# A two-layer GLA and neighbourhood-attention encoder: instructions ordered by a timeline simulation instead of the scheduler's own model

## The chip, the cores and the metric

The kernel runs on one core of a Trainium2 chip. The metric is the device time of one execution in microseconds; shorter is better. The core has TensorE (matmuls, PE in the profile; its weight loads are PEld), VectorE (DVE), ScalarE (ACT), GpSimd (POOL) and SyncE (SP), which issues nearly all DMA transfers here. Each engine works through its own list of instructions strictly in order; semaphores make it wait for other engines and for transfers. The kernel's operands, tiles and work are the same before and after the change; what differs is the order of each list.

## The reference

Two layers over 256 tokens and 16 meta tokens (272 in all), D = 2048, float32, batch 1. In each layer one projection gives the inputs of four GLA heads (bidirectional gated linear attention, 128 key and 256 value channels, chunks of 64) and of 16 heads of two-dimensional neighbourhood attention (NA, 64 channels, a window of 4 by 16 on a grid 64 wide, plus the meta tokens):

```python
proj = h @ w_in            # q,k,v,r,decay of GLA | q,k,v of NA
gla = _gla_mixer(q, k, v, r, gate_lr, w_up, b_up, norm_w)
na  = _na_mixer(nq, nk, nv, rel_bias)
h = _layer_norm(alpha * h + concat(gla, na) @ w_out, ln1_w, ln1_b)
h = _layer_norm(alpha * h + square(relu(h @ w_ff1)) @ w_ff2, ln2_w, ln2_b)
```

The MLP is 8192 wide. The meta tokens are dropped from the output, which is (1, 256, 2048).

## The kernel before

**Tiles and matmuls.** Activations lie transposed, 128 channels by 272 tokens, as 16 tiles x0 to x15 (y and u later on). Each float32 operand is split into a high part in the fast matmul format (fp32r) and a low rest; a product takes three matmuls (high by high, high by low, low by high), written as one of 512 columns and one of 256 where both parts of x lie beside each other. A weight tile is 128 x 1024 floats, 512 KB. L192 loads it on SP's queue into `raw` (3 buffers), L215 casts it to `wh` on ACT, L216 computes `wl` = raw - wh on DVE (4 buffers of each). `weights()` asks for tiles two ahead (`lead`), in the fixed order of `order()`. Some 770 tiles go through in all.

**Loops.** `by_m` walks over output tiles and accumulates over k in one PSUM bank (`eight`, L250, and `sixteen`, L262). `by_k` (L302, or `dense`, L312) walks over k and fills four or eight banks at once; layer 0 begins with it, two groups g of four banks for each k, since x arrives in pairs of tiles. There the program calls `load_x` for each pair (L431 loads `xraw`, 272 KB, 3 buffers; ACT and DVE split it). Layer 1 begins with it too, on the x that the second layer norm of layer 0 leaves.

**Side work.** GLA, NA, the layer norms and the gates are Python generators in two queues, `fg` and `bg`. After every group of main matmuls `pump` runs a step or more of them, so that their instructions are written between the main ones. In detail, as far as the steps below need it:

- Start: `load_gates` loads the decay weights (L451, two of 196 KB; L452, 256 KB), `consts` (L89 to L98) the vectors, identity and masks; L768 loads the bias `nb` of an NA pair of heads (352 KB), eight a layer.
- NA: softmax on ACT, DVE and POOL (L760 ends the meta tokens' part, `nms`), transposes by TensorE (L805, L806, L808), the product with v (L851, L858).
- GLA: L716 to L720 are the output matmuls, from `parts` (split by L337 on ACT and L338 on DVE) and `am` (L343).
- Layer norm: sums by TensorE (L983 makes one from `sp`), then `newton` (L576 to L578) makes `rs`, the reciprocal deviation; `ln_wide` (L1085) subtracts the mean `mu` and multiplies by `rs`, two tiles at a time; gain and bias follow on ACT (L1075) or POOL; `renew` splits the result into the next x (L337, L338). The first projections after it don't wait for it: they use the x from before the norm, and `fix` (L1121 to L1123) applies the norm to their result `fx`.
- End: `ln_out` turns the result back to tokens by rows: L1143 transposes (`turn`, four matmuls a block, eight blocks), L1156 the sums for each token, L1163 to L1167 and `newton` the deviation, L1148 subtracts the mean, L1182 scales and adds on DVE, and DMAs write the output.

**What sets the order.** The program's calls give each instruction a place in program order. The tile framework then schedules: it goes through the program with a model of how long things take, and picks for each engine which of the instructions whose inputs are ready in its model comes next, with program order as the tie-break. `issue_after` holds an instruction back until another one, here the last `wl` of the weights, has been placed; all side work and no transfer of `load_x`, L192 or L224 stands under it:

```python
raw = self.xr.tile([P, 2, L], F32, name="xraw", tag="xraw", bufs=3)      # L430
self.nc.sync.dma_start(raw, self.i["xT"][:, k:k + 2, :])                 # L431
...
with self.tc.issue_after(self.wl):                                       # in step()
    self.wants[q[0]] = bool(next(q[0]))
...
self.asked = nc.sync.dma_start(raw[:, c], ap[:, c]).ins                  # L192
self.nc.scalar.copy(h, r)                                                # L215
self.wl = self.nc.vector.tensor_tensor(lo, r, h.bitcast(F32), ALU.subtract).ins  # L216
```

Of the kernel before, what the change touches and what calls it, by code (L numbers as in the profile page):

```python
# [1259 lines left out]
def program(nc, arrays):  # L1260
    ins = {n: nc.dram_tensor(f"in_{n}", a.shape, mybir.dt.from_np(a.dtype), kind="ExternalInput").ap()
           for n, a in arrays.items()}
    out = nc.dram_tensor("out_0", (T, D), F32, kind="ExternalOutput").ap()
    with tile.TileContext(nc) as tc, ExitStack() as ctx:
        nc.scalar.preload_act_table_set("natural_log_exp_and_others")
        k = Trunk(ctx, tc, ins, out)
        for l in range(DEPTH):
            k.layer(l)
# [13 lines left out]
```

## Time and profile before

| | us |
|---|---|
| median of 3 runs | 2315.6 (2315.4 to 2317.69) |
| span of the profiled execution, the only time given of it | 2314.3 |
| busy: TensorE, VectorE, ScalarE, GpSimd | 2300.4, 1519.4, 1224.6, 160.4 |

The span runs from the first to the last instruction of the profiled execution and lies 1.3 us under the median. A row of a group or of the timeline reads: start in us (timeline only), duration in us, engine, line, operation, output <- inputs, shapes, how many in a row of that kind, and in brackets the idle time of the engine ahead of it and what ended it. Names carry no buffer numbers there. Adjacent matmuls overlap, so that a row's duration is longer than the time until the next one starts.

### The profile page before, as it was taken

How to read it: one execution, taken by the hardware profiler on the slowest of the kernel's cores; microseconds unless marked ns; L12 is line 12 of the kernel's file. 1: busy time of each engine (PE TensorE's matmuls, PEld its weight loads, DVE VectorE, ACT ScalarE, POOL GpSimd, SP SyncE). 2: the span in 40 equal slices, each digit the busy share in tenths (PEclk: the TensorE clock that was granted, in tenths of full speed). 3: DMA queues.
4: the chain of work that ended last, by engine and by line, in shares of the span. 5: the costliest groups of instructions: out<-in, count | busy, mean ns of one | idle time of the engine just before them, and what ended most of it. 6: DMA issues, size and time to landing. Idle time of an engine off the chain costs nothing.

```text
span 2314.3 us, 45228 instructions
## 1 busy us (share of the span) xinstructions
PE 2300.4 (99%) x18420; PEld 2186.8 (94%) x18420; DVE 1519.4 (66%) x2392; ACT 1224.6 (53%) x2096; POOL 160.4 (7%) x245
## 2 busy tenths in 40 slices
PE   9999999999999999999999999999999999999998
PEld 9999999999999999999999899989988888888888
DVE  5588778875544455547576788788866455666654
ACT  5666665564433344444456766655654334555443
POOL 0023210100000000000020122200100000000000
PEclk9999999999999999999999999999999999999999
DMA  8556665555566666555555566666666666666664
GB/s 263 162 164 185 200 197 177 174 180 177 181 182 178 179 181 181 177 181 181 177 179 165 174 180 204 213 185 191 188 192 193 196 189 195 193 193 221 194 199 138
DMA packets 129824, 431.65 MB, mean 187 GB/s; under 512 B 14792, under 2 KB 23496, under 8 KB 129616
## 3 DMA queue, kind: packets, MB, share of 16 engines
q1 hardware_dynamic: 127024, 421.95, 60.1%
q10 hardware_dynamic: 2592, 6.82, 0.8%
q8 instruction: 144, 2.36, 0.4%
q14 instruction: 64, 0.52, 0.1%
HBM read 420.32 MB, written 8.39 MB: 185 GB/s over the span
## 4 chain that ended last, share of the span: by engine, by line
PE 79%; DVE 3%; ACT 1%; issue 1%; DMA 0%; POOL 0%; DVEq 0%; ACTq 0%; POOLq 0%; SPq 0%
PE mm L250 44%; PE mm L262 30%; PE mm L302 2%; PE mm L312 1%; DVE wl L216 1%; PE bg L312 0%; ACT wh L215 0%; PE bg L302 0%; DMA raw<-in_win 0%; DVE acc L1085 0%; PE bg L851 0%; DVE S L615 0%; ACT ns L756 0%; PE bg L983 0%; PE bg L470 0%
## 5 line engine op out<-in xcount | busy, mean ns | idle before, releaser
L216 DVE TENSOR_TENSOR wl<-raw,wh 128x1024 fp32r<-128x1024 f32 (+1 forms) x770 | 936.3, 1223 | 619.8 <-ACT wh L215 518.4
L215 ACT CAST wh<-raw 128x1024 fp32r<-128x1024 f32 (+1 forms) x770 | 805.4, 1048 | 753.2 <-PE mm L250 360.1
L250 PE MATMUL mm<-x,wh 128*128 128x272 f32 (+3 forms) x4544 | 805.3, 294 | 0.0
L250 PEld LDWEIGHTS mm<-x,wh 128*128 128x128 f32 x4544 | 646.8, 188 | 15.4 <-DVE gtn L577 0.3
L250 PE MATMUL mm<-x,wl 128*128 128x272 f32 (+3 forms) x2432 | 519.6, 284 | 0.0
L250 PEld LDWEIGHTS mm<-x,wl 128*128 128x128 f32 x2432 | 390.8, 188 | 0.0
L250 PE MATMUL mm<-y,wh 128*128 128x272 f32 (+1 forms) x1440 | 235.0, 285 | 0.0
L250 PEld LDWEIGHTS mm<-y,wh 128*128 128x128 f32 x1440 | 199.7, 188 | 0.1
L262 PE MATMUL mm<-x,wh 128*128 128x512 f32 x832 | 193.8, 390 | 0.0
L262 PEld LDWEIGHTS mm<-x,wh 128*128 128x128 f32 x832 | 154.3, 188 | 31.0
L250 PE MATMUL mm<-u,wh 128*128 128x272 f32 (+1 forms) x1056 | 172.1, 285 | 0.0
L262 PE MATMUL mm<-y,wh 128*128 128x512 f32 x688 | 162.2, 389 | 0.0
L262 PEld LDWEIGHTS mm<-y,wh 128*128 128x128 f32 x688 | 128.7, 188 | 26.5
L250 PE MATMUL mm<-y,wl 128*128 128x272 f32 (+1 forms) x720 | 146.4, 284 | 0.0
L250 PEld LDWEIGHTS mm<-u,wh 128*128 128x128 f32 x1056 | 146.3, 188 | 0.0
L262 PE MATMUL mm<-u,wh 128*128 128x512 f32 x496 | 118.3, 391 | 0.0
L250 PEld LDWEIGHTS mm<-y,wl 128*128 128x128 f32 x720 | 112.5, 188 | 0.0
L262 PEld LDWEIGHTS mm<-u,wh 128*128 128x128 f32 x496 | 90.9, 188 | 17.7
L250 PE MATMUL mm<-u,wl 128*128 128x272 f32 (+1 forms) x528 | 107.3, 284 | 0.0
L262 PEld LDWEIGHTS mm<-x,wl 128*128 128x128 f32 x832 | 98.4, 188 | 2.0
L262 PE MATMUL mm<-x,wl 128*128 128x256 f32 x832 | 98.8, 276 | 0.0
L262 PEld LDWEIGHTS mm<-y,wl 128*128 128x128 f32 x688 | 84.2, 188 | 2.8
(285 smaller groups left out, 2288.7 us busy)
## 6 DMA issues: line engine op xcount, KB each, us to landing
raw<-in_wff SPq DMA_DIRECT2D x512, 512.0 KB, 3.8
raw<-in_win SPq DMA_DIRECT2D x190, 512.0 KB, 4.3
raw<-in_wout SPq DMA_DIRECT2D x64, 512.0 KB, 4.2
hop<-nt ACTq DMA_DIRECT2D x16, 384.0 KB, 2.3
np<-hop SPq DMA_DIRECT2D x64, 96.0 KB, 4.6
nb<-in_nab SPq DMA_DIRECT2D x16, 352.0 KB, 4.9
xraw<-in_xT SPq DMA_DIRECT2D x7, 272.0 KB, 5.5
out<-out SPq DMA_DIRECT2D x5, 256.0 KB, 3.4
```

Source lines behind the costliest of these rows:

```text
L215: self.nc.scalar.copy(h, r)
L216: self.wl = self.nc.vector.tensor_tensor(lo, r, h.bitcast(F32), ALU.subtract).ins
L250: mm(o, lhsT=self.block(w, j), rhs=rhs, start=first and not i, stop=last and i == len(TURNS[once]) - 1)
L262: self.nc.tensor.matmul(o, lhsT=self.block(both[j // 8][low], j % 8), rhs=rhs, start=first and not i + j, stop=bool(last and i and j == 15 ...
L302: self.nc.tensor.matmul(ps[g + m][:, :n], lhsT=self.block(parts[p][0], 4 * j + m if first else 2 * m + j), rhs=acts[k + j][parts[p][1]][:, ...
L312: self.nc.tensor.matmul(o, lhsT=self.block(both[low], i), rhs=rhs, start=not low and k + i % 2 == 0, stop=k == DC - 2 and i % 2 == 1 and n ...
```

## The change

One argument of the context under which the whole program is written:

```diff
-    with tile.TileContext(nc) as tc, ExitStack() as ctx:
+    with tile.TileContext(nc, schedule_with_timeline_sim=True) as tc, ExitStack() as ctx:
```

The scheduler now takes the times at which it thinks that engines are free and operands ready from a timeline simulation rather than from its own model. It still picks from the same instructions under the same dependencies. The lists of all engines differ from before, in places by a row, in places by dozens. Three places follow; a row is the line, the operation, output <- inputs with buffer numbers, the shape of the output, and xN for N equal ones in a row.

SyncE's queue at the start of the program, behind the transfers of the first tiles. Each `raw` of 128x1024 is one tile of weights: here those of k = 2, k = 4 and k = 6, two each (groups of banks 0 and 1). Before:

```order
L192 DMA raw<-in_win 128x1024
L431 DMA xraw<-in_xT 128x544
L192 DMA raw<-in_win 128x1024 x2
L431 DMA xraw<-in_xT 128x544
L192 DMA raw<-in_win 128x1024 x2
L431 DMA xraw<-in_xT 128x544
L192 DMA raw<-in_win 128x1024 x2
```

And now:

```order
L192 DMA raw<-in_win 128x1024
L431 DMA xraw<-in_xT 128x544 x3
L451 DMA gw_628<-in_wup 98x512
L192 DMA raw<-in_win 128x1024
L451 DMA gw_629<-in_wup 98x512
L452 DMA gw_630<-in_wlr 128x512
L89 DMA vec<-in_vec 128x2x66
L192 DMA raw<-in_win 128x1024
L91 DMA ident<-in_ident 128x128
L93 DMA sel<-in_sel 98x2
L95 DMA qmask<-in_qmask 16x48
L768 DMA nb<-in_nab 128x704
```

Behind these follow one `raw`, three more `xraw` and three `raw`; the first of those three is the first tile of k = 6. The gate weights, constants and `nb` stood behind all tiles of x before.

VectorE at the second layer norm of layer 0, up to the instruction that makes `rs` (L578). Before:

```order
L1058 TENSOR_TENSOR var_14829<-bg_14826,tn_14831 128x272
L1085 TENSOR_TENSOR acc_4774<-acc_4774,mu_14832 128x544
L1122 SCALAR_TENSOR_TENSOR fx_14877<-mu_14832,wb_14876,mm_14756 128x272
L576 SCALAR_TENSOR_TENSOR tn_14831<-var_14829,eps_656,rs_14830 128x272
L1085 TENSOR_TENSOR acc_4774<-acc_4774,mu_14832 128x544
L577 SCALAR_TENSOR_TENSOR tn_14831<-tn_14831,rs_14830 128x272
L1085 TENSOR_TENSOR acc_4774<-acc_4774,mu_14832 128x544
L578 SCALAR_TENSOR_TENSOR rs_14830<-tn_14831,rs_14830 128x272
L216 TENSOR_TENSOR wl_14929<-raw_14927,wh_14928 128x4x2x128
```

And now:

```order
L1085 TENSOR_TENSOR acc_4774<-acc_4774,mu_14832 128x544 x2
L1058 TENSOR_TENSOR var_14829<-bg_14826,tn_14831 128x272
L216 TENSOR_TENSOR wl_14929<-raw_14927,wh_14928 128x4x2x128
L1085 TENSOR_TENSOR acc_4774<-acc_4774,mu_14832 128x544
L576 SCALAR_TENSOR_TENSOR tn_14831<-var_14829,eps_656,rs_14830 128x272
L1121 COPY wb_14916<-mm_14845 128x2
L216 TENSOR_TENSOR wl_14963<-raw_14961,wh_14962 128x4x2x128
L1085 TENSOR_TENSOR acc_4774<-acc_4774,mu_14832 128x544
L577 SCALAR_TENSOR_TENSOR tn_14831<-tn_14831,rs_14830 128x272
L1122 SCALAR_TENSOR_TENSOR fx_14917<-mu_14832,wb_14916,mm_14845 128x272
L578 SCALAR_TENSOR_TENSOR rs_14830<-tn_14831,rs_14830 128x272
```

One more L1085 and one L1122 stand ahead of these rows, and L578 comes behind two low parts of weights (L216) that used to follow it.

TensorE in layer 0, where the main loop goes over y with `by_k` and L808 turns `nms`, the meta tokens' part of an NA pair. Before:

```order
L805 MATMUL bg<-ident,nv_2208 128x128 x2
L806 MATMUL bg<-ident,nr_2209 128x128
L302 MATMUL bg<-y_1925,wh 128x272 x2
L302 MATMUL bg<-y_2023,wh 128x272
L808 MATMUL bg<-ident,nms 128x128
L302 MATMUL bg<-y_2023,wh 128x272
L302 MATMUL bg<-y_1925,wl 128x272
```

And now:

```order
L302 MATMUL mm<-y_1925,wh 128x272 x2
L302 MATMUL mm<-y_2023,wh 128x272 x2
L302 MATMUL mm<-y_1925,wl 128x272
L808 MATMUL bg<-ident,nms 128x128
L302 MATMUL mm<-y_2023,wl 128x272
L851 MATMUL bg<-np,v_4817 64x128 x2
L851 MATMUL bg<-np,v_4816 64x128 x4
```

L808 now stands 27 main matmuls further back, just ahead of the L851 of the same head pair.

## The prediction

> **What bounds the kernel now.** I read the page first: busy time of the engines, and the chain of work that ended last.
>
> ```profile
> span 2314.3 us, 45228 instructions
> PE 2300.4 (99%) x18420; PEld 2186.8 (94%) x18420; DVE 1519.4 (66%) x2392; ACT 1224.6 (53%) x2096; POOL 160.4 (7%) x245
> PE 79%; DVE 3%; ACT 1%; issue 1%; DMA 0%; POOL 0%; DVEq 0%; ACTq 0%; POOLq 0%; SPq 0%
> ```
>
> TensorE is busy for 2300.4 of 2314.3 us, and the chain lies on it. So 13.9 us are all that a new order could win, unless it made the matmuls themselves shorter, and it changes none of them. The next view gives the busy time in stretches (columns: stretch, length, busy of the five engines with counts, granted clock, DMA share, GB/s).
>
> ```profile
> core 0: us, PE busy (x) PEld busy (x) DVE busy (x) ACT busy (x) POOL busy (x), PEclk, DMA share, GB/s
> 0.00:50.00 50.00, 48.79 (x379) 48.79 (x380) 27.26 (x38) 27.91 (x45) 3.15 (x18) 1.00 0.86 271
> 400.00:1200.00 800.00, 799.98 (x6528) 799.75 (x6527) 458.99 (x607) 362.09 (x508) 13.87 (x17) 1.00 0.60 180
> 2300.00:2314.00 14.00, 8.14 (x60) 7.01 (x58) 6.56 (x15) 3.23 (x8) 2.52 (x2) 0.97 0.41 150
> ```
>
> Of the 13.9 us, 1.21 lie before the first matmul and 5.9 in the last 14 us, behind the last matmul for the greater part. From 400 to 1200 us TensorE misses 0.02 us. The rest, some 6.8 us, is a dozen short gaps. A reordering of the long middle can win nothing there, and the question is whether it opens gaps. So I went through the places where TensorE has little in hand: the start, each gap, the two layer norms that feed a matmul, and the tail.
>
> **The change part by part: the start.** The order rows of the SyncE queue show that in front of the third pair of weight tiles (k = 6) now stand six xraw transfers instead of two, the three of the gate weights, vec, ident and the first nb.
>
> ```profile
> raw<-in_win SPq DMA_DIRECT2D x190, 512.0 KB, 4.3
> nb<-in_nab SPq DMA_DIRECT2D x16, 352.0 KB, 4.9
> xraw<-in_xT SPq DMA_DIRECT2D x7, 272.0 KB, 5.5
> ...
> gw<-in_wup SPq DMA_DIRECT2D x4, 196.0 KB
> raw<-in_win SPq DMA_DIRECT2D x3, 256.0 KB, 4.5
> ...
> head<-in_head SPq DMA_DIRECT2D x2, 264.0 KB, 2.9
> gw<-in_wlr SPq DMA_DIRECT2D x2, 256.0 KB, 5.6
> ```
>
> Up to and including the first tile of k = 6 the queue held: head 2 x 264, three raw of 256, five raw of 512, two xraw of 272; that is 4400 KB or 4.51 MB. Now it holds head 528, raw 768, raw 5 x 512, xraw 6 x 272, gate weights 196 + 196 + 256, vec and ident 66 + 64 (from their shapes) and nb 352: 6618 KB or 6.78 MB. When that tile came, and when TensorE wanted it:
>
> ```profile
> 11.61 1.05 ACT L215 CAST wh<-raw 128x1024 fp32r<-128x1024 f32 x1 [1.41 <-DMA raw<-in_win]
> ...
> 18.36 1.05 ACT L215 CAST wh<-raw 128x1024 fp32r<-128x1024 f32 x1 [1.10 <-DMA raw<-in_win]
> ...
> 23.05 0.65 PE L302 MATMUL mm<-x,wh 128*128 128x272 f32 x4
> ...
> 2.00:46.00 44.00, 44.00 (x345) 44.00 (x344) 24.94 (x36) 25.19 (x44) 1.68 (x11) 1.00 0.92 289
> 12.00:14.00 2.00, 2.00 (x18) 2.00 (x17) 1.23 (x1) 0.66 (x1) 0.00 (x0) 1.00 0.98 366
> ```
>
> The cast at 18.36 waited for this tile, so 4.51 MB had landed by then: counted from 2.0 us, 277 GB/s. The cast at 11.61 waited for the second tile of k = 2, which the rows place at 2.65 MB: 276 GB/s. The mean from 2 to 46 us is 289 GB/s at a DMA share of 0.92; scaled to a share of 1, that is 314, and I take 301, halfway between, as the quick end. The new landing is then 2.0 + 6.78 MB / 289 GB/s = 25.46 us, the cast of 1.05 ends at 26.5, and TensorE wants the tile at 23.05: **+3.5 us**, with 277 GB/s +4.5, with 301 +2.5. The second tile of k = 2 and both of k = 4 come some 0.4 to 0.7 us late by the same sum, which is part of the same lag. Behind k = 6 the lag does not grow: two tiles and an xraw (1.33 MB) in the 5.9 us of their 48 matmuls (0.1225 each, 799.98 us by 6528) are 225 GB/s, less than the queue carries. The gate weights, constants and nb that cause it are themselves wanted later; at their old places, behind the weights, they cost nothing.
>
> The Trainium skill speaks against this delay: DMA: Bandwidth & Descriptors, section "Where 436 GB/s comes from", puts the limit of one core's reads from HBM at about 358 GB/s, and by that figure as an estimate the tile would land at 20.9 us and be cast by 22.0, before it is wanted; no window over the whole start shows such a rate here, only the one at 12 us.
>
> **Second layer norm, 1195 to 1214 us.** DVE's order rows put two L1085, two L216, one L1121 and one L1122 more ahead of L578, which makes rs.
>
> ```profile
> 1195.47 0.72 DVE L1085 TENSOR_TENSOR acc<-acc,mu 128x544 f32<-128x544 f32 x1
> 1196.11 0.44 DVE L577 SCALAR_TENSOR_TENSOR tn<-tn,rs 128x272 f32<-128x272 f32 x1
> ...
> 1197.10 0.44 DVE L578 SCALAR_TENSOR_TENSOR rs<-tn,rs 128x272 f32<-128x272 f32 x1
> 1197.45 1.22 DVE L216 TENSOR_TENSOR wl<-raw,wh 128x1024 fp32r<-128x1024 f32 x1
> ...
> 1208.26 0.65 DVE L338 TENSOR_TENSOR x<-acc,x 128x272 fp32r<-128x272 f32 x1
> ...
> 1209.46 0.43 DVE L338 TENSOR_TENSOR x<-acc,x 128x272 fp32r<-128x272 f32 x1
> ...
> 1209.99 1.67 PE L302 MATMUL mm<-x,wh 128*128 128x272 f32 x12
> ...
> 1212.51 0.73 PE L302 MATMUL mm<-x,wh 128*128 128x272 f32 x4 [0.73 <-DVE fx L1122]
> ```
>
> An L1085 takes 0.64 us from its start to the next; two are 1.3, two L216 2.4, L1122 some 0.44 (the 128x272 shape of L578): 4.2 us, so rs ends at 1201.8, not 1197.5. Behind it stand two more L216, eight L1085, two L1123 and a copy (2.4 + 5.1 + 0.8 + 0.1): 8.4 us to 1210.2, then L338 of x1 and of x0. The low half of x0 is there at 1211.0 to 1211.35; TensorE, which starts this loop at 1209.99, wants x0 by its second matmul at 1210.1: 0.9 to 1.25. Then x2 comes another 0.7 to 0.9 late, behind an L216 and an L1122. Against 1.6 to 2.15 stands the present wait of 0.73 on L1122, which goes because the fourth bank's matmuls now stand later. **+1.2 net**; if ACT's and VectorE's queues run shorter than by these rows -0.7 (the wait goes and nothing comes), if all of rs's delay comes through +3.
>
> **1472 us, the GLA output matmuls of layer 1.**
>
> ```profile
> 1472.15 0.62 ACT L337 CAST parts<-A 128x512 fp32r<-128x512 f32 x1
> ...
> 1472.67 0.83 ACT L343 CAST am<-Am 16x256 fp32r<-16x256 f32 x2
> ...
> 1472.82 0.38 PE L716 MATMUL bg<-parts,V 128*128 128x256 f32 x1 [0.45 <-ACT parts L337]
> 1473.54 0.38 PE L717 MATMUL bg<-parts,V 128*128 128x256 f32 x1 [0.34 <-DVE parts L338]
> ```
>
> In ACT's new order a weight cast (1.05) and the two L343 (0.83) stand ahead of the cast of parts: it ends 1.88 later, while TensorE still reaches L716 at the same point. Four main matmuls now stand between L716 and L717, so the 0.34 goes. **+1.5**; nothing, if ACT is idle early enough to have both done.
>
> **Tail.** All sixteen L1143 transposes of the first four banks now precede L1156, where nine did.
>
> ```profile
> 2300.96 1.15 PE L1143 MATMUL mm<-ident,acc 128*128 128x128 f32 x9
> 2302.09 0.61 PE L1156 MATMUL bg<-ones,s 128*128 128x1 f32 x4
> ...
> 2305.17 1.54 DVE L1182 SCALAR_TENSOR_TENSOR out<-mm,rs,brow 128x256 f32<-128x256 f32 x3
> ```
>
> Nine transposes take 1.15 us or so, about 0.11 each beyond the first; seven more are 0.8. The chain L1156, var, rs, L1182 and the output transfers hang behind: **+0.7**, between 0 (VectorE's last L1011 ends at the same time as now) and 0.8.
>
> **What is won.** Five gaps in which TensorE waits, at places where the order changes:
>
> ```profile
> 217.56 0.33 PE L808 MATMUL bg<-ident,nms 128*128 128x128 f32 x1 [0.34 <-POOL nms L760]
> 340.92 0.33 PE L808 MATMUL bg<-ident,nms 128*128 128x128 f32 x1 [2.29 <-POOL nms L760]
> 1326.53 0.84 PE L983 MATMUL bg<-sp,ones 128*128 128x256 f32 x2 [0.54 <-ACT sp L337]
> 1507.59 0.73 PE L312 MATMUL mm<-y,wh 128*128 128x512 f32 x2 [0.90 <-DVE nr L541]
> 1516.04 0.87 PE L851 MATMUL bg<-np,v 64*64 64x128 f32 x20 [0.56 <-DVE v L812]
> ```
>
> The L808 at 340.92 moves behind 27 main matmuls that wait for nothing, 3.3 us at 0.1225 each, so its 2.29 goes. At 217.56 it moves by 1.3 us, at 1326.53 L983 moves by some 9 us, at 1507.59 the matmuls of the fourth bank go 13 places later, and at 1516.04 half of L851 goes later. The five are 2.29 + 0.34 + 0.54 + 0.90 + 0.56 = **-4.6**. What is late next is the matmul behind each; its operands are by the same rows there. If only half of it holds (a wait that moves instead of going), -2.3.
>
> **The sum.** 3.5 + 1.2 + 1.5 + 0.7 - 4.6 = +2.3 us on a span of 2314.3: 2316.6. The median of the runs before lies 1.3 above this span (2315.6), so the forecast is **2317.9 us**, one part in a thousand more. I left out two places of up to 0.5 together (L716 near 299 and 1370 us), and what the other 4,000 or so lines of difference between the orders may open: by 400 to 1200 us, where TensorE loses 0.02 us although VectorE and ScalarE work for half of the time, nothing; by the sum at 1210 us, met once more or twice, up to 4 us.
>
> **Rivals.** *The start is hidden.* The queue is fuller than now and carries more: the window at 12 us shows 366 GB/s at a share of 0.98. At that rate the tile is cast at 21.6 us and the 3.5 goes: -1.2, 2314.4 us. For it speaks the share of 0.86 in the first 50 us, against it that the two casts above waited for DMA at 276 and 277 GB/s.
>
> *The start costs twice as much, and the kernel is slower.* The transfers that are pulled forward have short rows: vec 264 bytes, ident 512, qmask and sel less. If these, or twelve transfers at once, bring the queue to 255 GB/s, the tile is cast at 2.0 + 26.6 + 1.05 = 29.6 us: +6.6, and the sum is +5.4, 2321.0 us. It decides from 263 GB/s down, only 5% under what the two casts show. Against it: 0.14 MB of 6.78 are in such rows.
>
> *The gaps go and nothing comes.* ACT and VectorE have idle time that covers the moves at 1210, 1472 us and the tail, and the start is hidden: -4.6 and the 0.7 at 1212: 2310.3 us. Against it stand the sums above, all of which would have to fail.
>
> That the option changes nothing is excluded: the rows of the instruction order differ on every engine.
>
> **How the numbers follow.** The forecast's case, +1 to +4 us, gets 0.44, the hidden start 0.18, the dear start 0.30, the clear gain 0.08. A measurement of this kernel can tell about 0.2%, 4.6 us: faster needs less than 2311.0, slower more than 2320.2. The clear gain alone is faster (0.08), the dear start is slower (0.30), the others within (0.62). The range leaves out the clear gain and the worst of the dear start with unseen gaps: 2313 to 2323 us.
>
> **What would show it.** Right: the first cast of k = 6 ends near 26.5 us and TensorE idles 3 to 4 us between 14 and 27 us; no gap at 341; a gap of 2 us at 1210 to 1214; one over 2 us at L716 near 1473; L1182 0.7 later against the last L250. Wrong: a DMA rate above 350 or below 263 GB/s from 2 to 25 us, or gaps of several us where I saw none, above all between 400 and 1200 us.

## The result, and the profile after

The changed kernel takes 2330.6 us (median of 5 runs, 2330.17 to 2332.95) against 2317.46 for the kernel before (5 runs on the same footing): a ratio of 1.0061, with a 95% interval of 1.005 to 1.0072. It is slower by some 13 us. The forecast was 2317.9 us in a range of 2313 to 2323, with 0.30 on slower.

The page's head of the profile after (span, busy time of each engine, shares of the chain that ended last):

```profile
span 2329.5 us, 45279 instructions
PE 2306.9 (99%) x18420; PEld 2192.2 (94%) x18420; DVE 1518.0 (65%) x2392; ACT 1223.1 (53%) x2096; POOL 175.1 (8%) x245
PE 93%; DVE 3%; DMA 2%; ACT 1%; issue 1%; POOL 0%; SPq 0%; DVEq 0%; ACTq 0%; POOLq 0%
```

The span grew by 15.2 us, from 2314.3. TensorE's idle time grew by 8.7 (22.6 instead of 13.9) and its busy time by 6.5, although it does the same 18420 matmuls. So the loss doesn't all stand in rows of waiting. Part of it lies within TensorE's busy time, which holds slower matmuls, and small waits too, since the ends of matmuls are modelled.

To see where, I numbered the main matmuls (L250, L262, L302, L312) of both traces from first to last, and took the difference of the starts of those of the same number: the lag of the changed kernel. Side work that moves past a point makes the lag jump for a moment and come back; what stays is real. It grows like this (us, worked out from the two traces, at the first main matmul from each time on):

| part of the program (time before) | lag at its end | growth | forecast for the part |
|---|---|---|---|
| start, to 25 | 2.0 | +2.0 | +3.5 |
| attention of layer 0, to 366 | 4.8 | +2.8 | -2.6 |
| feed-forward of layer 0, to 1200 | 4.9 | 0 | 0 |
| second layer norm, to 1250 | 6.8 | +1.9 | +1.2 |
| attention of layer 1, to 1540 | 5.2 | -1.6 | -0.5 |
| output projection of layer 1, 1540 to 1572 | 14.6 | **+9.4** | 0 |
| feed-forward of layer 1, to 2300 | 14.5 | -0.1 | 0 |
| tail (span less the last matmul) | 15.2 | +0.7 | +0.7 |

One place makes 9.4 of 15.2 (the expectations below, written with rougher figures, say 9.2, and 7.0 for the wait of 6.62). TensorE's timeline there, in the profile after:

```profile
1554.14 3.05 PE L262 MATMUL mm<-y,wl 128*128 128x256 f32 x25
1557.02 3.81 PE L262 MATMUL mm<-y,wh 128*128 128x512 f32 x16
1567.45 6.13 PE L262 MATMUL mm<-y,wh 128*128 128x512 f32 x16 [6.62 <-DVE acc L945]
1573.42 3.80 PE L262 MATMUL mm<-y,wl 128*128 128x256 f32 x32
```

Sixteen matmuls take 3.81 us; then TensorE waits 6.62 us for an L945 of VectorE; then the same sixteen take 6.13. The windows around it (columns as before) show why:

```profile
1555.00:1560.00 5.00, 5.00 (x34) 4.47 (x33) 5.00 (x10) 3.04 (x9) 0.00 (x0) 1.00 0.37 122
1560.00:1567.00 7.00, 0.83 (x4) 0.37 (x2) 7.00 (x20) 2.49 (x4) 0.00 (x0) 0.89 0.25 75
1567.00:1569.00 2.00, 1.55 (x4) 1.29 (x5) 2.00 (x4) 1.21 (x3) 0.00 (x0) 0.50 0.45 78
1569.00:1571.00 2.00, 2.00 (x6) 1.52 (x5) 2.00 (x8) 1.21 (x3) 0.00 (x0) 0.50 0.76 238
1571.00:1573.00 2.00, 2.00 (x8) 1.59 (x7) 1.98 (x6) 1.67 (x3) 0.00 (x0) 0.69 0.60 217
```

VectorE is busy all the time from 1555 to 1571. The granted clock of TensorE falls to 0.50 within the wait, at 1565.4 us, and stays there until 1572.2 (the trace records when it changes). What VectorE does meanwhile, from its timeline:

```profile
1555.73 0.76 DVE L1022 SCALAR_TENSOR_TENSOR acc<-acc,cs 128x256 f32<-128x256 f32 x2
1556.41 1.22 DVE L967 TENSOR_TENSOR acc<-acc,cs 128x1024 f32<-128x1024 f32 x1
1557.55 1.76 DVE L1022 SCALAR_TENSOR_TENSOR acc<-acc,cs 128x256 f32<-128x256 f32 x5
...
1560.50 1.09 DVE L1022 SCALAR_TENSOR_TENSOR acc<-acc,cs 128x256 f32<-128x256 f32 x3
1561.50 0.75 DVE L945 TENSOR_TENSOR acc<-acc,mm 128x256 f32<-128x256 f32 x2
...
1562.90 0.42 DVE L945 TENSOR_TENSOR acc<-acc,mm 128x256 f32<-128x256 f32 x1
...
1565.08 0.42 DVE L945 TENSOR_TENSOR acc<-acc,mm 128x256 f32<-128x256 f32 x1
...
1566.88 0.75 DVE L945 TENSOR_TENSOR acc<-acc,mm 128x256 f32<-128x256 f32 x2
```

Each output tile lies in one PSUM bank as two halves of 256 columns, and two L945 add them to `acc`; the bank comes free when the second has run. L945 comes behind the tile's L1022 (the shift by `cs`, the mean of the first four tiles), which all wait for `cs`. In the new order L1022 of ten tiles run first, then the first halves of four tiles, and only then a second half, at 1566.88. TensorE has four banks, has filled them by 1560.8 and stands. (The rows don't name the tile of an L945. But four tiles are complete at 1560.8, and TensorE starts again only at 1567.45, so the four L945 ahead of 1566.88 are one of each tile.) In the kernel before `cs` came at 1539.9, and L945 of a tile followed its L1022:

```profile
1540.12 0.76 DVE L1022 SCALAR_TENSOR_TENSOR acc<-acc,cs 128x256 f32<-128x256 f32 x2
1540.79 0.42 DVE L945 TENSOR_TENSOR acc<-acc,mm 128x256 f32<-128x256 f32 x1
1541.12 1.22 DVE L967 TENSOR_TENSOR acc<-acc,cs 128x1024 f32<-128x1024 f32 x1
1542.26 0.42 DVE L945 TENSOR_TENSOR acc<-acc,mm 128x256 f32<-128x256 f32 x1
```

In the new order `cs` came 16 us later than that, over 10 of them beyond the lag. TensorE's last L312 of the first tile group stand behind 23 of the next group's L262 (4.3 us), and the mean's L983 behind many more, at 1553 to 1554:

```profile
1536.24 3.57 PE L262 MATMUL mm<-y,wh 128*128 128x512 f32 x15
1539.64 1.08 PE L262 MATMUL mm<-y,wl 128*128 128x256 f32 x8
...
1541.94 1.07 PE L312 MATMUL mm<-y,wh 128*128 128x512 f32 x4
...
1553.32 0.28 PE L983 MATMUL bg<-sp,ones 128*128 128x256 f32 x1
```

### The profile page after: what moved, and what is told of

Read it like the earlier page. It is cut to its first block, busy times and chain, and to the rows that moved or that the text cites. A ratio compares the mean times of both kernels' runs of the same rounds, so it can differ in the third digit from the quotient of the medians.

```text
span 2329.5 us, 45279 instructions
## 1 busy us (share of the span) xinstructions
PE 2306.9 (99%) x18420; PEld 2192.2 (94%) x18420; DVE 1518.0 (65%) x2392; ACT 1223.1 (53%) x2096; POOL 175.1 (8%) x245
## 4 chain that ended last, share of the span: by engine, by line
PE 93%; DVE 3%; DMA 2%; ACT 1%; issue 1%; POOL 0%; SPq 0%; DVEq 0%; ACTq 0%; POOLq 0%
PE mm L250 56%; PE mm L262 29%; PE mm L302 3%; PE bg L302 1%; PE mm L312 1%; DVE wl L216 1%; DMA raw<-in_win 1%; ACT wh L215 0%; PE bg L851 0%; DMA np<-hop 0%; PE mm L778 0%; PE bg L629 0%; PE bg L470 0%; DVE acc L1085 0%; ACT ns L756 0%
## 5 line engine op out<-in xcount | busy, mean ns | idle before, releaser
L216 DVE TENSOR_TENSOR wl<-raw,wh 128x1024 fp32r<-128x1024 f32 (+1 forms) x770 | 937.6, 1224 | 650.5 <-ACT wh L215 539.4
L250 PE MATMUL mm<-x,wh 128*128 128x272 f32 (+3 forms) x4544 | 807.1, 294 | 0.0
L250 PEld LDWEIGHTS mm<-x,wh 128*128 128x128 f32 x4544 | 647.6, 188 | 15.5 <-issue 0.8
L250 PE MATMUL mm<-x,wl 128*128 128x272 f32 (+3 forms) x2432 | 520.4, 284 | 0.0
L250 PEld LDWEIGHTS mm<-x,wl 128*128 128x128 f32 x2432 | 391.1, 188 | 0.0
L250 PE MATMUL mm<-y,wh 128*128 128x272 f32 (+1 forms) x1440 | 234.6, 285 | 0.0
L250 PEld LDWEIGHTS mm<-y,wh 128*128 128x128 f32 x1440 | 199.6, 188 | 0.1
L262 PE MATMUL mm<-x,wh 128*128 128x512 f32 x832 | 193.8, 390 | 0.0
L262 PEld LDWEIGHTS mm<-x,wh 128*128 128x128 f32 x832 | 154.3, 188 | 31.0
L250 PE MATMUL mm<-u,wh 128*128 128x272 f32 (+1 forms) x1056 | 172.1, 285 | 0.0
L262 PE MATMUL mm<-y,wh 128*128 128x512 f32 x688 | 165.1, 393 | 6.6 <-DVE acc L945 6.6
L262 PEld LDWEIGHTS mm<-y,wh 128*128 128x128 f32 x688 | 130.1, 190 | 33.9 <-issue 7.0
L250 PE MATMUL mm<-y,wl 128*128 128x272 f32 (+1 forms) x720 | 146.4, 284 | 0.0
L250 PEld LDWEIGHTS mm<-u,wh 128*128 128x128 f32 x1056 | 146.3, 188 | 0.0
L262 PE MATMUL mm<-u,wh 128*128 128x512 f32 x496 | 118.6, 391 | 0.0
L250 PEld LDWEIGHTS mm<-y,wl 128*128 128x128 f32 x720 | 112.6, 188 | 0.0
L250 PE MATMUL mm<-u,wl 128*128 128x272 f32 (+1 forms) x528 | 107.5, 284 | 0.0
L262 PEld LDWEIGHTS mm<-u,wh 128*128 128x128 f32 x496 | 90.8, 188 | 17.7
L262 PEld LDWEIGHTS mm<-x,wl 128*128 128x128 f32 x832 | 98.4, 188 | 2.0
L262 PE MATMUL mm<-x,wl 128*128 128x256 f32 x832 | 98.8, 276 | 0.0
L262 PEld LDWEIGHTS mm<-y,wl 128*128 128x128 f32 x688 | 84.2, 188 | 2.9
```

Of the source, the lines that this page charges most:

```text
L250: mm(o, lhsT=self.block(w, j), rhs=rhs, start=first and not i, stop=last and i == len(TURNS[once]) - 1)
L262: self.nc.tensor.matmul(o, lhsT=self.block(both[j // 8][low], j % 8), rhs=rhs, start=first and not i + j, stop=bool(last and i and j == 15 ...
```

## The experiments

The question is whether the late sum, the burst on VectorE or both make the gap; whether the slow matmuls are the clock's; and what the other terms are worth. The kernel before took 2317.1 to 2317.6 (medians) beside these runs.

### The burst on VectorE, undone

```diff
             for part in ps:
-                tt(a, a, part, ALU.add)
+                end = tt(a, a, part, ALU.add).ins
             if k < DC - 1:
-                self.shift(k + 1, which)
+                with self.tc.issue_after(end): self.shift(k + 1, which)
```

> The changed kernel, with each L1022 (shift of the next tile) queued on VectorE behind the second L945 of the tile before. Theory 1 (the 7.0 us gap before the L262 at 1567 us needs both, the late sum cs and the burst of eleven L1022 and of first halves of L945 ahead of the second halves that free the banks): the gap goes to under 1 us, the half clock behind it goes too, 9.2 us in all, span 2320 us (2318.5 to 2322). Theory 2 (the late cs alone, which every L945 needs, makes the gap): the gap stays at 5 us or more, span 2327 or above. In both the start and the waits of L851 on np stay as they are.

2322.9 us (8 runs, 2321.6 to 2330.4), ratio 1.003 [1.002, 1.004]; span of the profile 2320.8. The gap and the half clock are gone: TensorE's rows run through.

```profile
1553.74 2.80 PE L262 MATMUL mm<-y,wl 128*128 128x256 f32 x23
1556.38 7.74 PE L262 MATMUL mm<-y,wh 128*128 128x512 f32 x32
1563.96 4.26 PE L262 MATMUL mm<-y,wl 128*128 128x256 f32 x32
```

The lag is 4.5 ahead of the place (at 1540) and 5.6 behind it. `cs` was still late here (its first L1022 runs at 1555.10), so theory 2 falls: the late sum alone makes no gap. The edit takes back the ten L1022 and the order of the halves together, and no run parts the two. In the changed kernel's rows the first L945 starts 0.7 us after the banks are full, and 5.4 us pass from it to the second half at 1566.88, so the order of the halves looks like the larger part.

### The late sum, undone

```diff
             for g in range(1, 4):
-                self.by_m(self.y, ...)
+                with self.tc.issue_after(self.dend) if last and g == 1 else ExitStack(): self.by_m(self.y, ...)
```

(`dend` is the last matmul of `dense`.)

> The changed kernel, with TensorE's first L262 of the output projection of layer 1 held behind the last L312 as in the kernel before; the burst of L1022 on VectorE stays (ten in a row ahead of the first L945). Theory 1 (both are needed): the sum cs is there some 8 to 10 us earlier, the burst ends before the four banks are full, the gap goes, span 2320 us (2318.5 to 2322). Theory 3 (the burst alone is enough): the gap stays at 4 us or more, span 2325 or above.

2325.3 us (7 runs, 2322.5 to 2329.6), ratio 1.0035 [1.0024, 1.0047]. With the lag taken off, the first L1022 runs 6 us earlier than in the changed kernel (1556.13 at a lag of 12 against 1555.73 at 5.4), less than the 8 to 10 expected. The burst of L1022 stayed, twelve with L967 between them, and the gap went all the same: the largest wait of TensorE from 1545 to 1590 is 0.74 us, and the lag grows by 1.4 there, not 9.4. So theory 3 falls too, and **both were needed**: the late sum put the burst into the last 5 us in which a bank had to come free. The profiled execution itself took 2327.7, because of two other stretches at half clock (357.2 to 364.0 and 1538.2 to 1545.0 us), behind waits of L851; the first of them:

```profile
352.00:354.00 2.00, 2.00 (x18) 2.00 (x18) 1.50 (x5) 0.96 (x5) 0.00 (x0) 1.00 0.90 296
354.00:356.00 2.00, 0.91 (x8) 0.69 (x6) 1.45 (x3) 0.89 (x1) 0.00 (x0) 1.00 1.04 250
356.00:358.00 2.00, 1.48 (x22) 1.32 (x24) 0.85 (x3) 0.39 (x2) 0.00 (x0) 0.80 0.55 172
358.00:360.00 2.00, 2.00 (x22) 1.96 (x19) 0.44 (x1) 0.39 (x1) 0.00 (x0) 0.50 0.50 195
```

Here one wait of 1.61 us, until 356.52, was enough.

### Is it the clock?

```diff
+                if not i + j: self.fill(x)
...
+        with self.tc.issue_after(self.last16):
+            o = self.bank()
+            for r in range(FILL):
+                self.nc.tensor.matmul(o, lhsT=x[0][0][:, :P], rhs=x[0].once, start=not r, stop=r == FILL - 1, skip_group_check=True)
```

(`fill` does this once, with FILL = 26, ahead of the fifth tile of the projection. Added lines shift the numbers: L262 is L263 here, L945 is L958 and L851 is L863; the 26 added matmuls are L277.)

> The changed kernel with 26 more matmuls of 512 columns into a spare bank, some 5.9 us, at the place where TensorE waits at 1560 us; nothing else is moved. If the 6.13 us (not 3.81) of the 16 matmuls behind the gap come from the clock, granted at 0.50 there because TensorE was idle for 6.6 us: the gap is filled, the clock stays at 1.00, the 16 take 3.8 us and the span falls by 2.3, to 2327.2 us. If they are slow because VectorE or the weights hold them up: they stay at 6 us and the span at 2329.5.

At the place it is as the first theory has it:

```profile
1561.35 6.05 PE L277 MATMUL bg<-y 128*128 128x512 f32 x26
1568.15 3.91 PE L263 MATMUL mm<-y,wh 128*128 128x512 f32 x16 [0.75 <-DVE acc L958]
```

The sixteen take 3.91 us instead of 6.13, at a granted clock of 1.00 throughout: 2.2 us of the 9.4 are the clock, and the wait itself is 6.6. The whole time did not fall, though: 2330.65 (4 runs, 2330.1 to 2334.3), the profiled span 2328.6. This execution ran at half clock from 357.8 to 361.2 us, behind waits of 0.65 and 0.54 at L851, where the changed kernel's profiled one, with waits of 1.48 and 0.21, did not. The price is shown at its place; in the total it was lost among such events.

### The start

```diff
-        self.nc.sync.dma_start(raw, self.i["xT"][:, k:k + 2, :])
+        with self.tc.issue_after(self.asked): self.nc.sync.dma_start(raw, self.i["xT"][:, k:k + 2, :])
```

and the same around `load_gates`, `consts` and the load of `nb`.

> The changed kernel with the transfers of xraw, gate weights, constants and nb held behind the weight tiles that precede them in the program, as in the kernel before. Theory: the main matmuls' lag of 2.0 us against the kernel before, which is there from 25 us on, goes to under 0.3, the gap of 0.90 at 15.7 us goes, span 2327.5 us. Rival (it is ScalarE's order of casts, not the transfers): a lag of 1 us or more stays at 25 us. The 7.0 us gap at 1567 stays in both.

2330.0 us (4 runs), span 2327.9. No wait is left between 5 and 60 us, and the lag at 25 us is 0.5, more than the theory's 0.3. That rest isn't the order's: the last kernel below (L805 to L808 one step later) has the kernel before's start and the same 0.5. In both the granted clock first rises late, at 6.8 and 7.0 us, against 5.8 in the kernel before. So in these two executions the delay goes with the transfers' order; of it 1.6 show in the span and 0.6 in the median, which one can't tell from nothing at this spread. Its size isn't fixed: in the six profiled executions with the new order at the start the lag at 25 us is 1.0 to 2.1, and the four edits together, which have the old order, show 1.7, behind a wait of 0.90 at 18.74.

### np ahead of the weights

The term that failed in layer 0 is at 356 us: TensorE's rows of the changed kernel, then SyncE's.

```profile
356.62 0.84 PE L851 MATMUL bg<-np,v 64*64 64x128 f32 x10 [1.48 <-DMA np<-hop]
357.66 0.55 PE L851 MATMUL bg<-np,v 64*64 64x128 f32 x8 [0.21 <-DMA np<-hop]
```

```profile
345.12 4.92 SPq L192 DMA_DIRECT2D raw<-in_wout  x3
350.73 2.51 SPq L826 DMA_DIRECT2D np<-hop  x4
353.34 3.44 SPq L192 DMA_DIRECT2D raw<-in_wout  x2
```

The load of `np` is issued at 350.73, behind weights; in the kernel before it was issued 6 us earlier:

```profile
344.74 2.71 SPq L826 DMA_DIRECT2D np<-hop  x4
```

```diff
-            self.asked = nc.sync.dma_start(raw[:, c], ap[:, c]).ins
+            with self.tc.issue_after(self.got): self.asked = nc.sync.dma_start(raw[:, c], ap[:, c]).ins
```

(`got` is the last issue of L826.)

> The changed kernel with each weight transfer L192 that the program asks for behind a fetch of np (L826) also queued behind it on SyncE, as the program has it; the last np of each layer then stands behind one weight tile fewer. Theory A (np is late because it stands behind a weight tile that waits for a free raw buffer): the waits of L851, 1.48 and 0.21 us at 356 us and 1.02 and 0.40 at 1534 us, fall to under 0.7 together at each place, span 2327.5 us. Theory B (softmax and hop of the last pair are late, whatever the queue): the waits stay within 0.5 us of these, span 2329.5.

2332.7 us (4 runs, 2331.8 to 2332.9), span 2331.0: slower, against both theories' totals. In layer 0 theory A holds: no wait of L851 is left at 356, and from 25 to 366 us the lag grows by 1.1 instead of 2.8. In layer 1 the edit turned the wait round: now the weights stood behind `np`.

```profile
1531.85 1.20 PE L312 MATMUL bg<-y,wh 128*128 128x512 f32 x4 [2.04 <-ACT wh L215]
```

ScalarE's cast for it had waited 4.11 us for its raw tile, and the clock fell to 0.50 at 1533.2 us. The gap at 1560 us cost more here too: the half clock behind it lasted 10.2 us instead of 6.8.

### Several edits together

The edits to the burst, the start, `np` and the late sum, in one kernel:

> The four edits together on the changed kernel: L1022 behind L945, the start's transfers behind the weights, np ahead of the weights, L262 behind the last L312. If the costs add up (8 to 9 us at 1555, 2.0 at the start, up to 1.5 by np): span 2318 us (2316.5 to 2320), and what is left over the kernel before lies at 220 to 300 us, at 356, at 1210 to 1232 us and in the tail. Rival (the order shifts and opens new gaps elsewhere): span 2321 or above, with a gap of over 2 us that the changed kernel didn't have.

2321.9 us (11 runs, 2320.9 to 2322.6), ratio 1.0022 [1.0013, 1.003], span 2320.4, between the two forecasts. The wait of L312 at 1530 us is here as well, 2.1 us, so the gap that the rival names came about, by an edit of mine. With `np` ahead in layer 0 alone:

> As the four edits together, but with np ahead of the weights in layer 0 alone, since in layer 1 that put the cast of a weight tile 2 us late (ACT waited 4.11 us for raw ahead of the L312 at 1531 us) and the clock fell behind it. If that wait was np's place in the queue: no wait over 0.5 us and no half clock at 1527 to 1536 us, span 2317 us (2316 to 2319). Rival (the weights are late there for another reason, the other edits' order): the wait of 2 us stays, span 2320 or above.

The profiled execution has the span and the clock of the first theory: 2317.2, and no stretch at reduced clock. The wait of 2 us is gone, though waits of 0.63 and 0.74 at L851 and 0.81 at L312 between 1529 and 1533 are over the 0.5 that it allowed. But this execution was not typical: 2322.2 in the median of 10 runs, 2318.8 to 2324.3. The mean clock of the runs is 0.999 in those under 2320 us and 0.998 in the others, so stretches at half clock are the likely difference; in which part of the program they lay isn't known, since only one execution has a trace. These edits bring back some 8 of the 13 us, and not all.

### The second layer norm

```diff
-        self.wl = self.nc.vector.tensor_tensor(lo, r, h.bitcast(F32), ALU.subtract).ins
+        with self.tc.issue_after(self.rsd): self.wl = self.nc.vector.tensor_tensor(lo, r, h.bitcast(F32), ALU.subtract).ins
```

(`rsd` is the layer norm's L578.)

> The changed kernel, with the weights' low parts L216 that the program writes behind a layer norm's L578 also queued behind it on VectorE. Theory (rs is late because two L216 and two more L1085 stand ahead of L578, and x0 and x2 are late by it): the waits of TensorE for L338, 1.09 us at 1216.4 and 1.03 at 1238.5, fall to under 0.4 together, and the main matmuls' lag behind the kernel before doesn't grow between 1190 and 1235 us (it grows by 1.9 in the changed kernel). Rival (the twelve L338 and the copies ahead of them on ScalarE are late by themselves, or the L216 that now stand behind are): waits of 1.5 us or more together stay there, or a wait for L216 takes their place.

2340.0 us (2 runs), span 2337.8: the rival. (By its row the changed kernel's second wait, at 1238.5, is 0.81 and not 1.03, and ends with L337 of ScalarE.) `rs` came earlier, at 1201.6 us instead of 1206.8, and yet x0 came later:

```profile
1217.82 1.01 PE L302 MATMUL mm<-x,wh 128*128 128x272 f32 x6 [1.75 <-DVE x L338]
1242.06 1.95 PE L302 MATMUL mm<-x,wh 128*128 128x272 f32 x7 [2.85 <-ACT x L337]
```

Six L216, eleven L1085 and six smaller instructions now stand between L578 and the first L338, which starts at 1217.3; in the changed kernel two, eight and three, and it starts at 1215.3. What decides is the whole row of work ahead of L338, not the place of L578 in it. The rest of this kernel's 9 us over the changed one isn't followed; half clock behind the wait of 2.85 and at 358 us is part of it.

### A better kernel: the wait at 341 us in the kernel before

The largest gap of the kernel before was L808 at 340.92, 2.29 us. Two edits of that kernel, with its own scheduler model. The first writes only L808 and the copies behind it later:

```diff
-        if self.full:
+        if self.full and c != 7:
             nc.tensor.transpose(pv[:, T + P:], meta.rearrange("p u c -> p (u c)"), self.ident)
...
         if c == 7:
+            if self.full:
+                nc.tensor.transpose(pv[:, T + P:], meta.rearrange("p u c -> p (u c)"), self.ident)
+                for hh, hs in enumerate(heads):
+                    nc.vector.tensor_copy(pm[hs, hh, :], pv[hs, T + P:T + P + NM])
             self.due.popleft()()
```

> The kernel before, with its own scheduler model, where the transpose L808 and the copies of the meta part for the last NA pair of layer 0 are written later in the program, just ahead of the L851 of the pair before. Theory: the gap of 2.29 us at 341 us goes and nothing comes, span 2312.0 us (2311.5 to 2313), 0.1% under the kernel before, and a steadier time, since no execution has the clock halved behind that gap. Rival (np or the copies are late next): a wait of 1 us or more ahead of L851 at 344 or 351 us, span 2313.5 or above.

2316.9 us (11 runs), ratio 0.9999 [0.999, 1.0007]: no change. L808 (L833 in this kernel) waits for a copy out of the same bank instead, and the clock behind it falls, as the row and three windows show:

```profile
342.69 0.30 PE L833 MATMUL bg<-ident,nms 128*128 128x128 f32 x1 [1.32 <-DVE v L812]
```

```profile
341.00:344.00 3.00, 1.64 (x28) 1.12 (x29) 2.50 (x7) 1.27 (x4) 0.00 (x0) 1.00 0.59 186
344.00:346.00 2.00, 2.00 (x27) 1.97 (x21) 1.87 (x3) 0.74 (x4) 0.00 (x0) 0.70 0.69 245
346.00:348.00 2.00, 2.00 (x10) 2.00 (x10) 1.00 (x4) 0.60 (x3) 0.00 (x0) 0.50 0.39 109
```

The second moves all four transposes one step later, and the store to `hop` one step earlier:

```diff
+        hop = self.hp.tile([P, 4, 192], F32, name="hop", tag="hop")
+        if c == 7 and self.full:
+            nc.scalar.dma_start(hop, turned)
+            yield True
         yield True
```

> The kernel before, with the transposes L805 to L808 of the last NA pair of layer 0 written one step later (and the store to hop one step earlier). Theory: nms is there when TensorE comes to L808, the gap of 2.29 us at 341 us goes, no clock falls behind it, span 2312.0 us (2311.5 to 2313.5) and a median some 2 to 3 us under the kernel before. Rival (v, np or the bank are late next, as in the edit that moved L808 alone, where L812 held it for 1.32 us): a wait of 1 us or more at 338 to 352 us, span 2313.5 or above.

**2314.0 us** (11 runs, 2313.0 to 2315.2) against 2317.1, ratio 0.9987 [0.9979, 0.9996]; span 2312.0. The gap is gone, and so is a spread: the kernel before lies between 2314.8 and 2318.8 in 20 runs, the nine with a mean clock of 1.000 all under 2316.6, ten of the eleven others over 2317. This is the fastest of all kernels here.

## Why the prediction was wrong

**What failed: the sum put at nothing what the other lines of difference open, with "up to 4 us" as the bound.** The gap at 1560 us is one of these, and it cost 9.4. I bounded it by the quiet of the stretch from 400 to 1200 us and by the price at the layer norm. At neither place did TensorE wait for a PSUM bank. In the output projection it did: four banks, and a drain that can't begin until a sum is there. The prediction followed VectorE's order only where TensorE waited already, so it missed that L945's second halves had moved behind ten L1022 and four first halves. The bound had the size of one wait, and no term for a clock that halves behind a wait; that alone was 2.2. Of the 12.9 us between the forecast for the span (+2.3) and the measurement (+15.2), 9.4 are this place and 5.4 the attention of layer 0; the other parts together came out some 2 lower than forecast.

**The gains, -4.6: half wrong, and the second step that failed.** L808 at 340.92 does lose its 2.29 us, as forecast (the lag falls by 2.5 at that matmul). But "its operands are by the same rows there" failed for the matmul behind it: the L851 of the last pair waits at 356 us for `np`, which SyncE issues 6 us later than before. The run with `np` ahead puts 1.7 us on that. The attention of layer 0 came out at +2.8 instead of -2.6, with further waits of 0.48 at L808 (221 us) and 0.88 at L716 (303 us), which I had put at a gain of 0.34 and at up to 0.5; the rest of this part isn't followed. In layer 1 most of the gains came (-1.6, against -0.5 with the 1.5 at 1472 us, which did not come), although L851 waits there too:

```profile
1534.14 0.44 PE L851 MATMUL bg<-np,v 64*64 64x128 f32 x4 [1.02 <-DMA np<-hop]
```

**The start, +3.5: right cause, too large, and another tile.** It is +2.0 in this execution, and goes with the transfers' order, as far as the run with the old order shows. The wait stands at the second tile of k = 2, whose cast starts 3 us later than before:

```profile
14.57 1.04 ACT L215 CAST wh<-raw 128x1024 fp32r<-128x1024 f32 x1 [0.67 <-DMA raw<-in_win]
15.67 2.25 PE L302 MATMUL bg<-x,wh 128*128 128x272 f32 x16 [0.90 <-ACT wh L215]
2.00:24.00 22.00, 21.10 (x152) 20.46 (x151) 12.32 (x24) 14.36 (x32) 1.36 (x10) 1.00 0.99 337
```

I had taken one rate, 289 GB/s, for the whole queue. Counted in the forecast's way, from 2.0 us to the start of a tile's cast and with all bytes up to the tile, the second tile of k = 2 came at 271 GB/s, those of k = 4 at 289 and 301, and the first of k = 6 at 311 or more. So the early tile cost 0.90, for which I had 0.4 to 0.7, and the tile of k = 6 was cast by 24.9 instead of 26.5 and cost some 0.4. Over the whole stretch the queue moved 337 GB/s at a DMA share of 0.99: as full as the rival of the hidden start said, though below its 366. (A slip of the forecast: 4.51 MB in the 16.36 us up to the cast at 18.36 are 275 GB/s, not 277; it changes no term of the sum.) The Trainium skill's limit of some 358 GB/s for one core's reads (DMA: Bandwidth & Descriptors, "Where 436 GB/s comes from") lies above what this stretch reached, and the delay was there.

**The layer norm, +1.2: right, 1.9.** `rs` ended at 1206.8, that is 4.4 later than before when the lag is taken off, against 4.2 forecast:

```profile
1206.33 0.44 DVE L578 SCALAR_TENSOR_TENSOR rs<-tn,rs 128x272 f32<-128x272 f32 x1
1216.36 1.02 PE L302 MATMUL mm<-x,wh 128*128 128x272 f32 x6 [1.09 <-DVE x L338]
```

TensorE waited 1.09 for x0 (0.9 to 1.25 forecast) and 0.81 for a later x, at 1238.5, behind L337 of ScalarE. The reason as I put it was too narrow: an early `rs` doesn't help while the same work stands behind it.

**1472 us, +1.5: not seen.** L716 and L717 wait for under 0.3 us each there instead of 0.45 and 0.34; ScalarE had time for the casts, the other end that I gave. **The tail, +0.7: right**, 0.7.

**The rivals.** The slower side had 0.30, for a dear start by a queue under 263 GB/s. The result was slower, and not by that mechanism.

## What to carry to other kernels

When an order is made anew by other times, compare it at every place where a buffer comes free late, not only where the bottleneck waits now: list for each pool of banks what must run before the freeing instruction, and count it against the time that the banks last. A wait that is removed on the bottleneck engine is won only if the next thing that it feeds, down to the queue of the load, isn't later too. And a wait of one to a few microseconds on TensorE is to be priced with the chance that the matmuls behind it run at half clock.

## What the hardware showed

TensorE's granted clock fell to 0.50 within or behind waits: at 1565.4 us, within the 6.62 us of the changed kernel, but also behind 2.04 at 1532 us (with `np` ahead), 1.61 at 356 (late sum undone), 1.32 at 343 (L808 alone moved) and 0.65 with 0.54 at 356 (wait filled). In the profiled execution of the kernel before, 2.29 us at 341 left it at 1.00, and so did 1.48 and 0.21 at 356 in the changed kernel.

The traces record when the granted clock changes. In each of the twelve executions it first rises 4.0 to 7.0 us after the start, and every later change lies a whole number of 3.413 us behind that rise; a stretch at half clock ahead of the program's end lasted 3.4, 6.8 or 10.2 us. So time falls into windows of 3.413 us, whose place differs from run to run, and a fall came at the end of a window in which TensorE had been idle for a third of the time or more. Of the windows at full clock (the last 20 us left out), all six in which TensorE was busy for some 40% or less were followed by half clock, six of the sixteen with 51 to 65%, and none with more. The 2.29 us of the kernel before lay 1.66 in one window and 0.63 in the next, and the first of these, busy for 51%, did not bring a fall. What decides between 51 and 65% stays open.

The Trainium skill, TensorE: Matmul & The Clock Gate, Part 1, tells of a gate that halves the clock after an idle window of some 3.4 us and runs freely against the program. The windows of 3.413 us, the 6.62 us and the event's chance from run to run agree with it. That a whole window must be idle doesn't: waits of 1.2 to 2.1 us were enough in five traces here.
